# Scores of two head pairs, their transposes and the stream's transposes each issued at one place in a two-layer decoder trunk

## The chip, the cores and the metric

The kernel runs on one core of one Trainium2 chip, as one program. The metric is the device time of one execution in microseconds (us); before the change three runs took 2105.35 to 2106.36 us, with a median of 2105.8. The engines have these names in the profile: PE is TensorE's matmuls, PEld its weight loads, DVE is VectorE, ACT is ScalarE, POOL is GpSimd, SP the queue that issues the weights' transfers. Each engine takes its instructions in the order in which the program gives them to it.

## The reference

Two layers act on 256 tokens of 2048 numbers, each with a token mixer and an MLP, both behind a normalisation and added to the stream. Float32 throughout.

```python
for i in range(2):
    h = rmsnorm(x, norm_mix[i])
    if i == 0:
        x = x + sliding_window_sink_attention(h, a_w_qkv[0], a_w_o[0], a_sinks[0])   # 32 heads, 4 key heads
    else:
        x = x + stick_breaking_attention(h, b_w_qkv[0], b_w_o[0])                     # 32 heads
    h = rmsnorm(x, norm_mlp[i])
    x = x + (relu(h @ w_in[i]) ** 2) @ w_out[i]                                        # hidden 8192
return rmsnorm(x, final_norm)

# mixer A, head h, 128-query blocks that see their own and the previous key block
s = q @ k.T / 8 - slope[h] * dist;  m = max(max(s), sink)
p = exp(s - m) / (sum(exp(s - m)) + exp(sink - m));  out = p @ v

# mixer B, strictly causal
z = q @ k.T / 8;  a[t, s] = sigmoid(z[t, s]) * prod_{s<j<t} (1 - sigmoid(z[t, j]));  out = a @ v
```

## The kernel before

Tokens lie in two tiles of 128 (`xt`), and a transposed, gain-scaled copy of the stream (`xg`, sixteen tiles of 128 features by 256 tokens) feeds the projections. Every float32 operand is held as a rounded high half and a low half, the difference; a product is the sum of three matmuls over the halves. All weights pass through one `WeightStream`: a 1 MB transfer from the SP queue into `wraw`, then for each half of it a cast on ScalarE (line 67, the high half of `wsplit`) and a subtraction on VectorE (line 75, the low half). TensorE runs through the weights in order.

The order on TensorE, ScalarE and VectorE is written out by hand. A projection (`proj`, `proj_v`, `proj_wide`) is a loop of steps; after each step it calls `between()`, which runs the stages that `plan((place, stage), ...)` put at this place, counted from the step after the call, and then `W.tick()`, which at every fourth step issues the cast of the weights ahead and one step later its subtraction. A step of `proj` is four matmuls, 16 steps make one projection; a place in `proj_wide` is three matmuls 512 wide. So attention, normalisation and transposes are woven into the stream of the next projections, and what a stage issues on ScalarE or VectorE stands in these engines' queues behind all that came at earlier places.

Attention A: eight groups (n = 0 to 7), each of two head pairs, four heads. A group's queries come from one projection; `summed` (ScalarE copies `low`, line 331, VectorE adds), the row scale (`qf`), and the split `qhl` follow. The scores of a pair (`pair_scores`, lines 381 and 383) fill two banks; VectorE adds the distance penalty while it reads them (`sc`, line 488) and finds the maxima (492 to 499); ScalarE takes the exponentials (`powers`, 506 and 509); VectorE sums up (`total`); ScalarE normalises (520). `turned` transposes a head's probabilities on TensorE (`transposed`, line 390) and splits them from the bank into `pTa` (ScalarE cast, then VectorE at the next place). `values` multiplies with `vpad` (539) and splits the result into `attnT`. Transposes and values of group n run during the projection of group n + 2 (`older`).

Attention B: eight groups j of two pairs. Values, keys and queries are projected one after another, 48 steps. `scores` adds the causal mask in the bank (639), `gates` takes two sigmoids of each head on ScalarE, `stick` makes the products along the keys on VectorE (two scans and two multiplications a head, 655 and 657), `turned` transposes and splits into `pT`, `values` multiplies (672 to 675).

At the end of each wide chunk (`ended`) the residual is added and the stream's four new tiles are transposed (`turn`, lines 227 to 232). `token_scale` makes the row scale, and its `spread` (272) multiplies it across the partitions.

PSUM is eight banks: four (`m`) for projections, four (`s`) handed out in rotation for scores, transposes, values and the spread. An instruction that writes a bank waits until what was in it has been read.

## Time and profile before

| | value |
|---|---|
| median of three runs | 2105.8 us |
| the profiled execution | 2106.19 us |
| its span in the profile | 2104.4 us |
| PE busy | 2077.8 us, 99% |
| PEld busy | 1760.6 us, 84% |
| DVE busy | 1303.8 us, 62% |
| ACT busy | 1094.5 us, 52% |
| mean granted clock of TensorE | 0.998 |
| 100 to 200 us (attention A): PE, DVE, ACT | 95.82, 79.73, 75.69 of 100 us |
| 700 to 800 us (MLP): PE, DVE, ACT | 100.00, 64.34, 55.52 of 100 us |
| 1100 to 1200 us (attention B): PE, DVE, ACT | 100.00, 83.17, 58.20 of 100 us |

Attention A lies from about 50 to 200 us of the span, the first MLP from 284 to 983, attention B from there to 1310, the second MLP from 1398 on. A busy PE means that some matmul was in flight; matmuls overlap, so their cost is read from the distance of their starts. The same holds on ScalarE and VectorE, where an instruction may start some 0.1 us before the one ahead has ended.

### The profile page before, as it was taken

The numbers are of one execution on the slowest core, as the hardware profiler recorded it, in microseconds if no ns is written. First come the engines' busy times: TensorE is split into PE (matmuls) and PEld (weight loads), VectorE is DVE, ScalarE is ACT, GpSimd is POOL, SyncE is SP. The second block draws the span as 40 slices with busy tenths as digits, with TensorE's granted clock in tenths as the row PEclk, the third lists the DMA queues.
The fourth block names the chain that finished last, engine by engine and source line by source line (L and its number), as shares of the span: only waits on it lengthen the run. The fifth ranks groups of instructions, "written<-read, shape, count | busy, mean of one in ns | idle before, by whom it ended". The sixth has DMA issues, their size and how long they took to land.

```text
span 2104.4 us, 27478 instructions
## 1 busy us (share of the span) xinstructions
PE 2077.8 (99%) x10994; PEld 1760.6 (84%) x10994; DVE 1303.8 (62%) x1845; ACT 1094.5 (52%) x1771; POOL 7.4 (0%) x17
## 2 busy tenths in 40 slices
PE   8999999999999999999999999999999999999998
PEld 7777888888888888888888888888888888888886
DVE  5887566664446665555778788566664445665454
ACT  6776555553335554444555555455553335554443
POOL 0000000000000000000000000000000000000000
PEclk9999999999999999999999999999999999999999
DMA  8555866565565566555544554566656566566553
GB/s 228 133 121 121 185 196 197 182 199 187 196 196 181 184 200 194 186 181 195 165 162 158 168 166 147 189 193 199 188 183 205 186 198 187 180 193 200 192 189 119
DMA packets 340464, 380.37 MB, mean 181 GB/s; under 512 B 72624, under 2 KB 257008, under 8 KB 340208
## 3 DMA queue, kind: packets, MB, share of 16 engines
q1 hardware_dynamic: 339760, 376.50, 58.4%
q8 instruction: 86, 1.41, 0.3%
q10 hardware_dynamic: 576, 2.11, 0.2%
q14 instruction: 42, 0.34, 0.1%
HBM read 376.49 MB, written 2.10 MB: 180 GB/s over the span
## 4 chain that ended last, share of the span: by engine, by line
PE 91%; DVE 4%; ACT 3%; DMA 1%; issue 1%; SPq 0%; ACTq 0%; DVEq 0%
PE m L291 43%; PE m L300 41%; PE m L323 5%; DVE wsplit L75 1%; DMA wraw<-in_a_w_qkv_dram 1%; ACT sc L520 1%; ACT wsplit L67 1%; ACT sc L506 1%; PE s L390 1%; PE s L227 0%; DVE sc L488 0%; PE s L381 0%; DVE mx L492 0%; PE s L672 0%; DVE t L333 0%
## 5 line engine op out<-in xcount | busy, mean ns | idle before, releaser
L75 DVE TENSOR_TENSOR wsplit<-wraw,wsplit 128x1024 fp32r<-128x1024 f32 x712 | 857.8, 1223 | 531.2 <-ACT wsplit L67 530.8
L67 ACT CAST wsplit<-wraw 128x1024 fp32r<-128x1024 f32 x712 | 732.6, 1051 | 581.1 <-PE m L300 421.9
L291 PE MATMUL m<-xg,wsplit 128*128 128x256 f32 (+1 forms) x5696 | 1016.5, 338 | 3.3 <-DVE wsplit L75 2.8
L291 PEld LDWEIGHTS m<-xg,wsplit 128*128 128x128 f32 x5696 | 861.5, 188 | 125.5 <-DVE wsplit L75 3.2
L300 PE MATMUL m<-wsplit,h 128*128 128x512 f32 x3072 | 699.9, 389 | 0.0
L300 PEld LDWEIGHTS m<-wsplit,h 128*128 128x128 f32 x3072 | 575.7, 188 | 119.0
L300 PE MATMUL m<-wsplit,attnT 128*128 128x512 f32 x768 | 184.6, 395 | 0.0
L300 PEld LDWEIGHTS m<-wsplit,attnT 128*128 128x128 f32 x768 | 142.2, 189 | 28.2 <-issue 0.2
L341 DVE TENSOR_TENSOR h<-hsq,h 128x256 fp32r<-128x256 f32 x128 | 54.5, 425 | 118.1 <-ACT h L338 118.1
L331 ACT COPY low<-m 128x256 f32<-128x256 f32 x178 | 63.4, 370 | 122.7 <-PE m L291 122.5
L577 ACT ACTIVATE hsq<-t 128x256 f32<-128x256 f32 x128 | 53.5, 418 | 126.7 <-DVE t L575 126.7
L333 DVE TENSOR_TENSOR t<-m,low 128x256 f32<-128x256 f32 x178 | 73.0, 421 | 62.3 <-ACT low L331 62.2
L323 PE MATMUL m<-wsplit,xg 128*128 128x256 f32 (+1 forms) x576 | 110.8, 343 | 0.0
L323 PEld LDWEIGHTS m<-wsplit,xg 128*128 128x128 f32 x576 | 85.1, 188 | 11.4
L575 DVE SCALAR_TENSOR_TENSOR t<-t,rbc 128x256 f32<-128x256 f32 x128 | 54.4, 425 | 4.4
L338 ACT CAST h<-hsq 128x256 fp32r<-128x256 f32 x128 | 52.0, 406 | 4.1
L229 ACT ACTIVATE xg<-s,gains 128x256 fp32r<-128x256 f32 x64 | 28.6, 474 | 31.0 <-PE s L227 30.7
L232 DVE SCALAR_TENSOR_TENSOR xg<-s,gains,xg 128x256 fp32r<-128x256 f32 x64 | 29.3, 480 | 23.0 <-ACT xg L229 23.0
L506 ACT ACTIVATE sc<-sc,nm 128x256 f32<-128x256 f32 x64 | 28.4, 445 | 23.0 <-DVE nm L497 22.3
L366 DVE TENSOR_TENSOR xt<-m,xt 128x512 f32<-128x512 f32 x46 | 29.8, 684 | 15.6 <-PE m L300 15.6
L243 ACT ACTIVATE junk<-xt 128x512 f32<-128x512 f32 x40 | 25.1, 628 | 23.0 <-DVE xt L366 11.5
L655 DVE TENSOR_TENSOR_SCAN rest<-keep 128x256 f32<-128x256 f32 x64 | 35.3, 551 | 0.0
(106 smaller groups left out, 641.0 us busy)
## 6 DMA issues: line engine op xcount, KB each, us to landing
wraw<-in_mlp_w_in_dram SPq DMA_DIRECT2D x128, 1024.0 KB, 5.7
wraw<-in_mlp_w_out_dram SPq DMA_DIRECT2D x128, 1024.0 KB, 5.0
wraw<-in_b_w_qkv_dram SPq DMA_DIRECT2D x48, 1024.0 KB, 5.0
wraw<-in_a_w_qkv_dram SPq DMA_DIRECT2D x64, 256.0 KB, 3.9
wraw<-in_a_w_o_dram SPq DMA_DIRECT2D x32, 512.0 KB, 7.0
wraw<-in_b_w_o_dram SPq DMA_DIRECT2D x16, 1024.0 KB, 5.0
wraw<-in_a_w_qkv_dram SPq DMA_DIRECT2D x3, 1024.0 KB, 10.0
xt<-in_x_dram SPq DMA_DIRECT2D x4, 256.0 KB, 4.8
```

Of the source, the lines that this page charges most:

```text
L67: self.nc.scalar.copy(out=wt[:, 0], in_=raw)
L75: self.nc.vector.tensor_tensor(out=wt[:, 1], in0=raw, in1=wt[:, 0].bitcast(F32), op=ALU.subtract)
L291: nc.tensor.matmul(banks[j][:, :cols], lhsT=wt[:, u, kt % UK, j * P : (j + 1) * P], rhs=act[:, kt, : cols // S, :], start=(kt == 0 and u = ...
L300: nc.tensor.matmul(banks[tt], lhsT=act[:, kt, a, tt * P : (tt + 1) * P], rhs=wt[:, w, kt % 2, :], start=(first and n == 0), stop=(last and ...
L323: nc.tensor.matmul(banks[tt][:, :cols], lhsT=act[:, kt, u, tt * P : (tt + 1) * P], rhs=wt[:, : cols // S, kt % UK, :], start=(kt == 0 and ...
L331: nc.scalar.copy(out=low, in_=b[:, S:])
L333: nc.vector.tensor_add(out=t, in0=b[:, :S], in1=low)
L338: nc.scalar.copy(out=hi, in_=src)
L341: nc.vector.tensor_tensor(out=lo, in0=src, in1=hi.bitcast(F32), op=ALU.subtract)
L506: nc.scalar.activation(out=sc[:, hh, cols], in_=sc[:, hh, cols], func=AF.Exp, bias=nm[:, hh, blk : blk + 1], scale=1.0, accum_out=den[:, h ...
L575: nc.vector.scalar_tensor_tensor(out=t, in0=t, scalar=0.0, in1=scale["row"], op0=ALU.max, op1=ALU.mult)
L577: nc.scalar.activation(out=sq, in_=t, func=AF.Square)
```

## The change

Five things are rearranged, and no arithmetic is added or taken away.

1. `pair_scores` takes both pairs: the split products of both, then the full-precision products of both. It allocates four banks at once. In A the scores of both pairs stand at place 5 (before: 3 and 6, both 3 in the last group); `scores` is divided into `distances`, which runs at once for both pairs, and `maxima`, at places 6 and 7. In B the scores stand at place 4 (before 3 and 4, both 3 in the last group).
2. The four transposes of a group's probabilities stand at one place: in A at 9 (before 1, 1, 7, 8), in B at 18 (before 12, 13, 18, 20). Values: A 14 as before, B both at 24 (before 20, 24).
3. Four stream tiles are transposed at one place of the next chunk, 4 (before one each at 3, 4, 5, 6), two to a bank; at the start two each at places 0 to 5 (before one each at 0 to 11).
4. The last groups' places are further apart: A own transposes at 15 and values at 20 (before 10, 12, 13, 13 and 18); B 14 and 20 (before 11, 12, 15, 16 and 16, 18).
5. The spread stands five places after the row scale (before four).

The core of the diff:

```diff
-    def turn(dt, gain, wait):
-        b = bank("s", 4)
-        for tt in range(2):
-            nc.tensor.transpose(b[:, tt * P : (tt + 1) * P], xt[tt][:, dt * P : (dt + 1) * P], ident)
...
+    def turn(dts, gain, wait):
+        banks = [bank("s", 4) for _ in dts[::2]]
+        parts = [banks[n // 2][:, n % 2 * S : n % 2 * S + S] for n in range(len(dts))]
+        for dt, b in zip(dts, parts):
+            for tt in range(2):
+                nc.tensor.transpose(b[:, tt * P : (tt + 1) * P], xt[tt][:, dt * P : (dt + 1) * P], ident)
...
+            if wait:
+                plan((n // 2, lambda dt=dt, b=b: low(dt, b)))
...
-        plan((4, spread))
+        plan((5, spread))
...
-        for n in range(4):
-            plan((3 + n, lambda n=n: turn(4 * c + n, gain, True)))
-        plan((2, lambda: square(0, c)), (4, lambda: square(1, c)))
+        plan((2, lambda: square(0, c)), (3, lambda: square(1, c)),
+             (4, lambda: turn(range(4 * c, 4 * c + 4), gain, True)))
...
+    def pair_scores(*pairs):
+        banks = [[bank("s", 4) for _ in range(2)] for _ in pairs]
+        rows = [slice(hh * HD, (hh + 1) * HD) for hh in range(2)]
+        for (qf, q, kf, k), bs in zip(pairs, banks):
+            for n, (u, v) in enumerate(((0, 0), (1, 0), (0, 1))):
+                for r, b in zip(rows, bs):
+                    nc.tensor.matmul(b[:, :S], lhsT=q[r, u, P:], rhs=k[r, v, :], start=(n == 0), stop=(n == 2))
+        for (qf, q, kf, k), bs in zip(pairs, banks):
+            for r, b in zip(rows, bs):
+                nc.tensor.matmul(b[:, S : S + P], lhsT=qf[r, :P], rhs=kf[r, :P], start=True, stop=True)
+        return banks
...
             if older:
-                plan(*zip((1, 1, 7, 8, 14) if n < 7 else (0, 3, 3, 6, 12), older))
+                plan(*zip((9, 14), older))
+            plan((5, scores))
             if n < 7:
-                plan(*zip((3, 6, 7, 13), pair[0][0]), *zip((6, 10, 13, 14), pair[1][0]))
+                plan(*zip((6, 8, 9, 12), pair[0][1]), *zip((7, 11, 13, 15), pair[1][1]))
             else:
-                plan(*zip((3, 4, 5, 6), pair[0][0]), *zip((3, 6, 8, 11), pair[1][0]), *zip((10, 12, 13, 13, 18), late))
+                plan(*zip((6, 7, 8, 10), pair[0][1]), *zip((7, 9, 11, 12), pair[1][1]), *zip((15, 20), late))
...
+            plan((4, scores))
             if j < 7:
-                plan(*zip((3, 5, 9, 10, 12, 13, 20), a), *zip((4, 9, 12, 12, 18, 20, 24), b))
+                plan(*zip((5, 9, 10), pairs[0][1]), *zip((9, 12, 13), pairs[1][1]), (18, turns), (24, both_values))
             else:
-                plan(*zip((3, 5, 5, 6, 11, 12, 16), a), *zip((3, 5, 7, 9, 15, 16, 18), b))
+                plan(*zip((5, 7, 8), pairs[0][1]), *zip((6, 9, 10), pairs[1][1]), (14, turns), (20, both_values))
```

What it does to the queues, first on ScalarE in a middle group of attention A. Before, from one group's `low` on, the rows are (`L338` are splits, `L67` weight casts, `L506` exponentials of the first pair):

```order
L331 COPY low<-m 128x256 x2
L338 CAST qhl<-qf 128x256 x2
L67 CAST wsplit<-wraw 128x1024
L338 CAST pTa<-s 128x3x128 x2
L67 CAST wsplit<-wraw 128x1024
L506 ACTIVATE sc,den<-sc,nm 128x256
L506 ACTIVATE sc,den<-sc,nm 128x128
L506 ACTIVATE sc,den<-sc,nm 128x256
L506 ACTIVATE sc,den<-sc,nm 128x128
L509 ACTIVATE es<-es 128x4
L338 CAST pTa<-s 128x3x128 x2
L67 CAST wsplit<-wraw 128x1024
```

and now, with the lines renumbered (`L341` splits, `L513` exponentials):

```order
L334 COPY low<-m 128x256 x2
L341 CAST qhl<-qf 128x256 x2
L67 CAST wsplit<-wraw 128x1024 x2
L513 ACTIVATE sc,den<-sc,nm 128x256
L513 ACTIVATE sc,den<-sc,nm 128x128
L513 ACTIVATE sc,den<-sc,nm 128x256
L513 ACTIVATE sc,den<-sc,nm 128x128
L516 ACTIVATE es<-es 128x4
L67 CAST wsplit<-wraw 128x1024
L341 CAST pTa<-s 128x3x128 x4
```

Two probability casts stood ahead of the second weight cast and two behind the exponentials; now all four stand behind the exponentials and one more weight cast.

On VectorE in the same group before (`L75` low halves of weights, `L488` distance passes, `L492` to `L499` maxima, `L341` low halves of probabilities):

```order
L75 TENSOR_TENSOR wsplit<-wraw,wsplit 128x1024
L341 TENSOR_TENSOR pTa<-s,pTa 128x3x128 x2
L488 SCALAR_TENSOR_TENSOR sc<-dist,s 128x384 x2
L492 TENSOR_REDUCE mx<-sc 128x6
L493 TENSOR_TENSOR mx<-mx 128x2
L497 SCALAR_TENSOR_TENSOR nm<-mx,nsinks 128x4
L499 TENSOR_TENSOR es<-nm,nsinks 128x4
L75 TENSOR_TENSOR wsplit<-wraw,wsplit 128x1024
L488 SCALAR_TENSOR_TENSOR sc<-dist,s 128x384 x2
L492 TENSOR_REDUCE mx<-sc 128x6
```

and now (`L492` distance passes, `L499` to `L506` maxima):

```order
L75 TENSOR_TENSOR wsplit<-wraw,wsplit 128x1024
L492 SCALAR_TENSOR_TENSOR sc<-dist,s 128x384 x4
L75 TENSOR_TENSOR wsplit<-wraw,wsplit 128x1024
L499 TENSOR_REDUCE mx<-sc 128x6
L500 TENSOR_TENSOR mx<-mx 128x2
L504 SCALAR_TENSOR_TENSOR nm<-mx,nsinks 128x4
L506 TENSOR_TENSOR es<-nm,nsinks 128x4
L499 TENSOR_REDUCE mx<-sc 128x6
L500 TENSOR_TENSOR mx<-mx 128x2
L504 SCALAR_TENSOR_TENSOR nm<-mx,nsinks 128x4
L506 TENSOR_TENSOR es<-nm,nsinks 128x4
L520 TENSOR_TENSOR den<-den,es 128x4
```

Four distance passes and a weight half stand ahead of the first maximum, and the probabilities' low halves, ahead of the distances before, come three rows after the last one shown.

On TensorE at the end of attention B before (`L381` and `L383` scores, `L390` transposes, `L672` values, `L300` the output projection):

```order
L300 MATMUL m<-wsplit,attnT 128x512 x12
L381 MATMUL s<-khl,qhl 128x256 x6
L383 MATMUL s<-kf,qf 128x128 x2
L381 MATMUL s<-khl,qhl 128x256 x6
L383 MATMUL s<-kf,qf 128x128 x2
L300 MATMUL m<-wsplit,attnT 128x512 x24
L390 MATMUL s<-ident,beta 128x128 x3
L300 MATMUL m<-wsplit,attnT 128x512 x3
L390 MATMUL s<-ident,beta 128x128 x3
L300 MATMUL m<-wsplit,attnT 128x512 x9
L390 MATMUL s<-ident,beta 128x128 x3
L300 MATMUL m<-wsplit,attnT 128x512 x3
```

and now (`L385` and `L388` scores, `L395` transposes, `L690` values, `L303` the output projection):

```order
L303 MATMUL m<-wsplit,attnT 128x512 x15
L385 MATMUL s<-khl,qhl 128x256 x12
L388 MATMUL s<-kf,qf 128x128 x4
L303 MATMUL m<-wsplit,attnT 128x512 x30
L395 MATMUL s<-ident,beta 128x128 x12
L303 MATMUL m<-wsplit,attnT 128x512 x18
L690 MATMUL s<-pT,vpad_8158 128x512
```

The four transposes of probabilities stand together behind thirty matmuls, and the values eighteen later.

## Rows read from the trace of the kernel before

**Rows 1.** Waits of TensorE: waiter, releaser, us in total, times, longest.
```profile
PE s L381 <- ACT qhl L338: 4.1, 7, 1.2
...
PE s L672 <- DVE pT L341: 1.2, 1, 1.2
...
PE s L272 <- DVE diag L267: 0.7, 2, 0.4
```

**Rows 2.** Timeline of one group of attention A: start, duration, engine, line, instruction.
```profile
101.93 0.62 ACT L331 COPY low<-m 128x256 f32<-128x256 f32 x2
...
104.08 1.04 ACT L67 CAST wsplit<-wraw 128x1024 fp32r<-128x1024 f32 x1
...
105.15 1.23 DVE L75 TENSOR_TENSOR wsplit<-wraw,wsplit 128x1024 fp32r<-128x1024 f32 x1 [0.52 <-ACT wsplit L67]
...
106.30 1.01 DVE L341 TENSOR_TENSOR pTa<-s,pTa 128x384 fp32r<-128x384 f32 x2
107.23 1.01 DVE L488 SCALAR_TENSOR_TENSOR sc<-dist,s 128x384 f32<-128x384 f32 x2
...
109.65 0.51 ACT L506 ACTIVATE sc<-sc,nm 128x256 f32<-128x256 f32 x1 [2.83 <-DVE nm L497]
...
111.52 0.83 ACT L338 CAST pTa<-s 128x384 fp32r<-128x384 f32 x2
...
112.25 1.05 ACT L67 CAST wsplit<-wraw 128x1024 fp32r<-128x1024 f32 x1
...
115.30 1.03 ACT L67 CAST wsplit<-wraw 128x1024 fp32r<-128x1024 f32 x1
...
117.63 0.56 ACT L338 CAST attnT<-s 128x512 fp32r<-128x512 f32 x1
118.10 1.49 ACT L520 ACTIVATE sc<-sc,den 128x256 f32<-128x256 f32 x4
...
119.50 0.62 ACT L331 COPY low<-m 128x256 f32<-128x256 f32 x2
```

**Rows 3.** Chain of waits, MLP stretches: start, duration, what, count.
```profile
1567.57 174.09 PE m L300 x768
1741.66 178.35 PE m L291 x1024
```

**Rows 4.** Stretches: length, busy (x count) of PE, PEld, DVE, ACT, POOL, PEclk, DMA.
```profile
174.00:178.00 4.00, 2.35 (x17) 1.79 (x19) 3.09 (x6) 1.50 (x5) 0.00 (x0) 0.91 0.24 46
178.00:182.00 4.00, 4.00 (x19) 3.13 (x16) 3.76 (x12) 2.90 (x10) 0.00 (x0) 0.67 0.00 0
1304.00:1308.00 4.00, 2.81 (x18) 2.15 (x17) 3.97 (x7) 0.48 (x1) 0.00 (x0) 1.00 0.05 19
```

**Rows 5.** TensorE's timeline in a group of attention B, scores.
```profile
1020.35 0.63 PE L381 MATMUL s<-khl,qhl 64*128 64x256 f32 x6
...
1022.03 0.62 PE L381 MATMUL s<-khl,qhl 64*128 64x256 f32 x6
```

**Rows 6.** Timeline at the end of attention B, TensorE.
```profile
1293.86 0.62 PE L381 MATMUL s<-khl,qhl 64*128 64x256 f32 x6
...
1300.78 0.49 PE L390 MATMUL s<-ident,beta 128*128 128x128 f32 x3
```

**Rows 7.** TensorE's timeline in the output projection of attention A.
```profile
189.63 0.82 PE L390 MATMUL s<-ident,sc 128*128 128x128 f32 x6
...
193.70 2.25 PE L539 MATMUL s<-pTa,vpad 128*128 128x512 f32 x12
...
207.37 0.38 PE L227 MATMUL s<-ident,xt 128*128 128x128 f32 x2
...
208.30 0.38 PE L227 MATMUL s<-ident,xt 128*128 128x128 f32 x2
```

**Rows 8.** Timeline at the end of attention B, VectorE.
```profile
1296.81 0.69 DVE L655 TENSOR_TENSOR_SCAN rest<-keep 128x256 f32<-128x256 f32 x1
...
1298.54 1.22 DVE L75 TENSOR_TENSOR wsplit<-wraw,wsplit 128x1024 fp32r<-128x1024 f32 x1
```

More of the change, by code (lines that the diff above doesn't have):

```diff
@@ L468, in trunk_kernel @@
             gains_in(0)
[L469 to L471 removed]
+            turn(range(4), 0, False)
+            plan(*[(n, lambda n=n: turn(range(4 + 2 * n, 6 + 2 * n), 0, True)) for n in range(6)],
                  *[(12 + c, lambda c=c: square(0, c)) for c in range(4)])
@@ L483, in head_pair, with distances @@
             blocks = (slice(0, S), slice(S, S + P))
-            def scores():
+            def distances(banks):
                 sc = st["sc"] = tmp.tile([P, 2, 3 * P], F32, name="sc", bufs=4)
-                for hh, b in enumerate(pair_scores(qf, q, kf[:, gp, :], k[:, gp])):
+                for hh, b in enumerate(banks):
                     nc.vector.scalar_tensor_tensor(out=sc[:, hh, :], in0=dist,
@@ L524, in turned @@
                 transposed(st["sc"][:, hh, :], pTs[hh][:, 0, :, u, :], pTs[hh][:, 1, :, u, :])
-            return (scores, powers, total, normalise), turned
+            return distances, (maxima, powers, total, normalise), turned
         def values(pTs, gp, i):
@@ L680, in values @@
                      (1, lambda: split(attnT[:, 2 * j + u, 0, :], attnT[:, 2 * j + u, 1, :], t, 0)))
-            return scores, gates, lambda: stick(0), lambda: stick(1), lambda: turned(0), lambda: turned(1), values
+            return masked, (gates, lambda: stick(0), lambda: stick(1)), turned, values
         for j in range(8):
@@ L690, in trunk_kernel, with scores, turns, both_values @@
             qs = scaled(tmp, proj(NDT, xg), r8, "q")
-            a, b = [head_pair(j, u, ks[u], qs[u]) for u in range(2)]
+            pairs = [head_pair(j, u) for u in range(2)]
+            def scores(ks=ks, qs=qs, pairs=pairs):
+                made = pair_scores(*[(*qt, *kt) for qt, kt in zip(qs, ks)])
+                for (masked, _, _, _), banks in zip(pairs, made):
+                    masked(banks)
+            def turns(pairs=pairs):
+                for _, _, turned, _ in pairs:
+                    for hh in range(2):
+                        turned(hh)
+            def both_values(pairs=pairs):
+                for _, _, _, values in pairs:
+                    values()
+            plan((4, scores))
             if j < 7:
-                plan(*zip((3, 5, 9, 10, 12, 13, 20), a), *zip((4, 9, 12, 12, 18, 20, 24), b))
+                plan(*zip((5, 9, 10), pairs[0][1]), *zip((9, 12, 13), pairs[1][1]), (18, turns), (24, both_values))
             else:
-                plan(*zip((3, 5, 5, 6, 11, 12, 16), a), *zip((3, 5, 7, 9, 15, 16, 18), b))
+                plan(*zip((5, 7, 8), pairs[0][1]), *zip((6, 9, 10), pairs[1][1]), (14, turns), (20, both_values))
         out_proj(attnT, 3)
```

48 lines of the change are left out of this document (22 added, 26 removed).

## The prediction

> **What bounds the kernel now.** I read the slices of the page first: TensorE is busy and at full granted clock in every slice, so most of the span is a matmul stream with other work beside it. The waits of TensorE come next [rows 1]: few and short, and the only repeated one stands in attention A, where the scores wait for the split queries seven times. Then one group of A in time order [rows 2]: the same ScalarE copy (`low`) stands at 101.93 and at 119.50, so a group lasts 17.57 us. TensorE's own work does not fill that: sixteen steps of four matmuls at 178.35/256 = 0.697 [rows 3] are 11.15, four score and transpose insertions and one set of value products about 5.5, together 16.7. The rows name what does fill it: each starts where one before it ended, ScalarE and VectorE in turn. In A the group is a closed loop through the two in-order queues of ScalarE and VectorE, and TensorE has 0.9 us to spare. In the MLPs and in attention B the opposite holds: 768 matmuls in 174.09 us without a break [rows 3], and in the steady B loop no wait at all (the 1.2 us for `pT` [rows 1] is the end of B).
>
> **Group A, which decides.** The change lets both pairs' scores, all four distance passes and then both maxima go one after the other on VectorE, and puts all four probability casts in one block on ScalarE, behind the first pair's exponentials. No instruction is added or removed there; what changes is who stands behind whom. I rebuild the loop from [rows 2] in the new order, from `low` to the next `low`: to the first weight cast 104.08 - 101.93 = 2.15; until its VectorE half 1.07; that half 1.15; four distance passes at the rate of two 384-wide passes in 107.23 - 106.30 = 0.93, so 1.86; the next weight half, which stands between them and the maxima, 1.15; maxima until the exponentials, 109.65 - 107.23 less two passes, 1.49; exponentials of the first pair 111.52 - 109.65 = 1.87; a weight cast, 117.63 - 115.30 = 2.33 less the four normalisations 119.50 - 118.10 = 1.40, so 0.93; four probability casts at 0.73 for two, 1.46; exponentials of the second pair 1.87; normalisation and weight cast 2.33; `attnT` cast 0.47; second normalisation 1.40. Sum 19.20, against 17.57: +1.63 a group. Before, two of the casts stood early, while ScalarE had nothing to do until the maxima, and the second pair's distances and maxima ran beside the first pair's exponentials; now ScalarE idles over all four distance passes and then has 3.3 us of queue before the second pair's exponentials. Six such loops give +9.8. The first has no older probabilities (1.46 + 0.47 less), its excess lies between 0 and 1.6, I take 0.8: **+10.6**.
>
> Does TensorE hide it? The values at place 14 need the third low half of the probabilities. Counted from `low`: exponentials end at 10.74, the weight cast's half may start at 11.81, ends at 12.96, three lows end at about 14.4. TensorE leaves the previous values (1.75 after their wait) at 14.4 + 1.75 - 19.2 = -3.0, seven steps (4.88) bring it to the scores at 1.8, which end at about 3.4; nine steps and twelve transposes (6.27 + 1.32) bring it to the values at 11.0. It waits there about 3 us, with two matmuls in between. The old wait of the scores for the split queries goes (most of the 4.1 us in [rows 1]), but a new one of the values for VectorE's `pTa` is late next, and longer. Behind the waiting value product stand the rest of its own matmuls, a step, and the next group's scores, which still arrive 1.0 before VectorE can take them (4.37): so the loop, not TensorE, keeps the time.
>
> **End of A.** Before, the stretch 174 to 178 had TensorE idle for 4.00 - 2.35 = 1.65 and the clock's fall cost (1 - 0.91) x 4 + (1 - 0.67) x 4 = 1.7 [rows 4]; both go with the later scores. New: the older values wait about 2.4 by the same queue; and the transposes of the fourth own head take, by the rotation of four banks, the bank of those values, whose low half on VectorE waits behind a weight half; that ends near 19.7 where TensorE is there at 17.2, so 2.6. +5.0 - 3.35 - 0.5 for merged insertions = +1.1; bounds -2 and +3, the bank order being read from the code alone; I take **+0.8**.
>
> **The merged insertions.** One pair's scores: 1022.03 - 1020.35 less one step 0.70 = 0.98 [rows 5]; two pairs at once: 1300.78 - 1293.86 less 24 x 174.09/768 = 5.44, so 1.48 [rows 6]. Merging saves 0.48 wherever TensorE keeps the time: not in A. Six transposes cost 193.70 - 189.63 less 15 x 0.227 = 0.67, two cost 208.30 - 207.37 less 0.68 = 0.25 [rows 7]: 0.11 each and 0.01 to 0.03 for entering. So grouping transposes saves next to nothing: eight together 0.89 against 1.00, for twelve ends of wide chunks 1.3 by the rounded rows, of which I take **-1.0**. The run of six in these rows costs no more for each transpose than the run of two, so no clock was lost over it. The Trainium skill ("TensorE: Matmul & The Clock Gate", Part 4: PE-mode transpose) says otherwise: that the full clock does not engage for transposes, and that one took about 275 ns in a kernel's context. By that figure twelve are, as an estimate, 3.3 us where the rows give 1.3; what the rule would do here is rival four.
>
> **Start and row scales.** Six insertions of four transposes for twelve of two save about 0.3; the tiles turned earlier also spare TensorE a wait for a late half. Bounds -2 and +0.5, I take -0.7. The sums' spread, one place later, gets 0.7 us more cover: the two waits of 0.7 in all [rows 1] go. Together **-1.4**.
>
> **Group B.** Merged scores save 0.48 a group. The transposes move from places 12 to 20 to place 18, the values to 24. VectorE after the scores: four masks (1.4, an estimate at the 384-wide rate scaled down), four weight halves 4.6, four sticks at 1298.54 - 1296.81 = 1.73 [rows 8] 6.9, the two value inputs and their halves with one wait for ScalarE 2.5, then the first low half 0.5: 15.9. TensorE reaches the values after 20 x 0.697 + 1.32 = 15.3. A new wait of about 0.5 eats the 0.48: **0**, bounds -3.5 (no wait) and +3.5 (a wait of 1). In the last group the transposes come ten places of 0.68 after the scores, at 6.8, and the fourth is at the array at 8.0, but the fourth stick ends at 1.3 + 2 x 1.15 + 6.9 = 10.5: a wait of 2.6, in place of the 1.2 of [rows 1]: +1.4, merging -0.2, **+1.2**.
>
> **The clock.** It fell once, from 2.4 to 1.2 GHz, after TensorE had stood idle for 1.65 of 4 us, and it did not at the end of B, after 1.19 of idling [rows 4]. The new waits are longer than both. A fall costs 1.7 of TensorE's time; in the A loop 1.0 of it is covered, so 0.7 each. Six there and three at the ends are between 0 and +9.3; when a fall comes I can't tell, I take **+2**.
>
> Sum: 10.6 + 0.8 - 1.0 - 1.4 + 0 + 1.2 + 2 = **+12.2**. The profiled execution took 2106.2 us (span 2104.4), 0.4 above the median; so 2118.4 on its own, 2118.0 for a median.
>
> **Rivals.**
> One, faster: the A loop is closed by TensorE after all, at 11.15 + 1.48 + 1.32 + 2.1 = 16.05, because the new order lets the two queues run ahead. Then A gains 1.5 x 7, B 0.48 x 7, start and turns 2.4: 2090. The 4.1 us that go [rows 1] speak for it; against it, TensorE already had spare time while the loop took 17.57. It decides if the values do not wait. Chance 0.07.
> Two, about the same: the A loop grows by only half (part of the casts slips into ScalarE's idle time), B's values don't wait: +5.3 - 3.4 + 0.6 = 2108.5. The long idle of ScalarE before its exponentials speaks for it; the order of the queue against. 0.15.
> Three, much slower: the clock falls at every new wait, +9.3 in place of +2: 2125. For it, the new waits are longer than the one at which it fell; against it, each is split by two matmuls. 0.20.
> Four, slower still: a run of twelve transposes brings the clock down by itself. There are eight such runs in B, where nothing covers a fall: 8 x 1.7 = 13.6 more, 2132. Against it stands the run of six [rows 7]. 0.03. This is what the Trainium skill's section on transposes, cited above, would do here.
>
> **How the numbers follow.** The forecast keeps 0.55, with its own range 2112 to 2123. The range runs from 2107 to 2127: it holds the forecast, rival three and most of two, and leaves out one, four and the ends of the others, about 0.18. What a measurement of this kernel can tell from no change is 0.2%, 4.2 us: slower than 2110.0 is the forecast, rival three and a small part of two, 0.80; faster than 2101.6 is rival one and a little, 0.08; between, 0.12.
>
> **What would show it.** After: `low` to `low` in A at 19 rather than 17.6; TensorE waiting for `pTa` in the line of the value products, six or seven times, 2 to 3.5 each, and no longer for `qhl`; in B nothing over 1 until the last group, where transposes wait for `beta`. A period of 17.6 or less, or value products that start at once, would make it wrong; so would B groups shorter than before by 0.4 or more.

## The result, and the profile after

The changed kernel takes 2121.7 us (median of four runs, 2121.12 to 2121.94) against 2105.9 in the same measurement: ratio 1.0075, 95% interval 1.0064 to 1.0087. It is slower, 3.7 us more than the forecast and inside its own range. The profiled execution has a span of 2120.0 us, 15.7 more than before, at a mean granted clock of 0.993 (0.998).

Where it went can be read exactly, since the matmuls on the weights' stream are the same 10112 in the same order in both traces. The starts of the same matmul, after less before, at the borders of the stages:

| stage | us longer (after less before) | forecast |
|---|---|---|
| up to the first product | +1.49 | start -0.7 |
| keys and values of A | -0.56 | |
| the eight query projections, with A's loop woven in | +13.84 | +10.6, and most of the clock's +2 |
| first chunk of A's output projection | +2.03 | +0.8 |
| from there to the first product of B | -1.17 | chunk ends -1.0, spread -0.7 (both layers) |
| B, eight groups | -0.93 | 0 |
| first chunk of B's output projection | +1.18 | +1.2 |
| the rest | -0.22 | (chunk ends, as above) |
| sum (before rounding) | +15.67 | +12.2 |

TensorE's waits after (waiter, releaser, us in total, times, longest), to be held against [rows 1]:

```profile
PE s L546 <- DVE pTa L344: 10.9, 11, 2.0
...
PE m L294 <- DVE wsplit L75: 4.3, 1, 4.3
PE s L385 <- ACT qhl L341: 3.2, 1, 3.2
PE s L395 <- DVE attnT L344: 2.6, 1, 2.6
PE s L395 <- DVE beta L675: 2.3, 1, 2.3
```

The seven waits of the scores for `qhl` are down to one; eleven records of value products that wait for `pTa` stand in their place. The wait at the start has grown from 2.8 to 4.3, the one at the end of B from 1.2 to 2.3, and at the end of A there is a new one of 2.6. A middle group of A, the counterpart of [rows 2]:

```profile
89.34 0.63 ACT L334 COPY low<-m 128x256 f32<-128x256 f32 x2
...
93.72 1.94 DVE L492 SCALAR_TENSOR_TENSOR sc<-dist,s 128x384 f32<-128x384 f32 x4
...
98.08 0.51 ACT L513 ACTIVATE sc<-sc,nm 128x256 f32<-128x256 f32 x1 [4.59 <-DVE nm L504]
...
100.89 1.59 ACT L341 CAST pTa<-s 128x384 fp32r<-128x384 f32 x4
...
102.37 0.52 ACT L513 ACTIVATE sc<-sc,nm 128x256 f32<-128x256 f32 x1
...
102.86 0.59 PE L546 MATMUL s<-pTa,vpad 128*128 128x512 f32 x2 [1.98 <-DVE pTa L344]
...
108.43 0.64 ACT L334 COPY low<-m 128x256 f32<-128x256 f32 x2
```

From `low` to `low` 19.09, where it was 17.57. The first exponentials (`L513`) start 8.74 after `low`; before it was 7.72. Ahead of them VectorE makes four distance passes (93.72), behind them stand a weight cast, all four probability casts (100.89) and only then the second pair's exponentials (102.37). TensorE waits 1.98 for the casts' low halves at its value products (102.86). All eight `low` stand at 51.94, 70.27, 89.34, 108.43, 128.01, 147.60, 166.70 and 186.16. From the second `low` on these are six steady loops; the first group is a case of its own. Three of the six are 19.07 to 19.10, three 19.46 to 19.59; in each of these three the clock fell once (near 122.2, 142.7 and 180.2). Stretches (length, PE, PEld, DVE, ACT, POOL busy with counts, granted clock, DMA):

```profile
118.00:122.00 4.00, 2.02 (x12) 1.44 (x11) 2.93 (x9) 4.00 (x15) 0.00 (x0) 1.00 0.31 69
122.00:126.00 4.00, 3.92 (x13) 3.00 (x14) 1.76 (x6) 3.75 (x13) 0.00 (x0) 0.57 0.96 218
207.50:211.00 3.50, 3.50 (x10) 2.71 (x9) 1.96 (x3) 0.94 (x1) 0.00 (x0) 0.51 0.94 229
1000.00:1300.00 300.00, 299.73 (x1843) 259.78 (x1842) 238.54 (x425) 172.59 (x308) 2.19 (x2) 1.00 0.51 165
```

After TensorE had been busy for 2.02 of 4 us the clock was at 1.2 GHz for most of the next four (0.57), and so again at the end of A (0.51). In B it stays at 1.00.

### The profile page after: what moved, and what is told of

Same layout as the page of the kernel before. It is cut to its first block, busy times and chain, and to the rows that moved or that the text cites. A ratio compares the mean times of both kernels' runs of the same rounds, so it can differ in the third digit from the quotient of the medians.

```text
span 2120.0 us, 27530 instructions
## 1 busy us (share of the span) xinstructions
PE 2080.4 (98%) x10994; PEld 1768.5 (83%) x10994; DVE 1301.1 (61%) x1845; ACT 1093.9 (52%) x1771; POOL 7.4 (0%) x17
## 4 chain that ended last, share of the span: by engine, by line
PE 92%; ACT 3%; DVE 3%; issue 1%; DMA 0%; SPq 0%; ACTq 0%; DVEq 0%
PE m L294 43%; PE m L303 40%; PE m L326 5%; DVE wsplit L75 1%; ACT sc L513 1%; ACT wsplit L67 1%; ACT sc L527 1%; PE s L230 1%; DVE sc L492 1%; PE s L546 1%; PE s L690 0%; PE s L395 0%; PE s L385 0%; DVE mx L499 0%; DVE t L336 0%
## 5 line engine op out<-in xcount | busy, mean ns | idle before, releaser
L75 DVE TENSOR_TENSOR wsplit<-wraw,wsplit 128x1024 fp32r<-128x1024 f32 x712 | 857.2, 1223 | 535.5 <-ACT wsplit L67 527.5
L67 ACT CAST wsplit<-wraw 128x1024 fp32r<-128x1024 f32 x712 | 731.4, 1052 | 575.2 <-PE m L303 422.8
L303 PE MATMUL m<-wsplit,h 128*128 128x512 f32 x3072 | 697.8, 389 | 0.0
L303 PEld LDWEIGHTS m<-wsplit,h 128*128 128x128 f32 x3072 | 576.4, 188 | 119.6
L303 PE MATMUL m<-wsplit,attnT 128*128 128x512 f32 x768 | 179.6, 393 | 0.0
L303 PEld LDWEIGHTS m<-wsplit,attnT 128*128 128x128 f32 x768 | 144.4, 189 | 29.9
L326 PE MATMUL m<-wsplit,xg 128*128 128x256 f32 (+1 forms) x576 | 104.7, 339 | 0.0
L341 ACT CAST h<-hsq 128x256 fp32r<-128x256 f32 x128 | 52.0, 406 | 4.1
L513 ACT ACTIVATE sc<-sc,nm 128x256 f32<-128x256 f32 x64 | 28.4, 450 | 37.2 <-DVE nm L504 37.2
L546 PE MATMUL s<-pTa,vpad 128*128 128x512 f32 (+1 forms) x96 | 24.6, 406 | 11.0 <-DVE pTa L344 10.9
```

The source lines that it names most:

```text
L67: self.nc.scalar.copy(out=wt[:, 0], in_=raw)
L75: self.nc.vector.tensor_tensor(out=wt[:, 1], in0=raw, in1=wt[:, 0].bitcast(F32), op=ALU.subtract)
L303: nc.tensor.matmul(banks[tt], lhsT=act[:, kt, a, tt * P : (tt + 1) * P], rhs=wt[:, w, kt % 2, :], start=(first and n == 0), stop=(last and ...
L326: nc.tensor.matmul(banks[tt][:, :cols], lhsT=act[:, kt, u, tt * P : (tt + 1) * P], rhs=wt[:, : cols // S, kt % UK, :], start=(kt == 0 and ...
L341: nc.scalar.copy(out=hi, in_=src)
L513: nc.scalar.activation(out=sc[:, hh, cols], in_=sc[:, hh, cols], func=AF.Exp, bias=nm[:, hh, blk : blk + 1], scale=1.0, accum_out=den[:, h ...
```

## The experiments

The theory: in attention A the order of work in the queues of ScalarE and VectorE closes the loop, and everything TensorE does or waits for there follows from it. The rivals: the falls of the clock and TensorE's waits make the loss; or the merged blocks themselves (twelve transposes, four banks at once) do. Up to the run on the start and the ends, the edits shown are against the changed kernel, from there on against the run before; "..." marks lines left out. "Period" is the time from `low` to `low` in the steady groups.

**A's order of before.**

```diff
...
-                plan(*zip((9, 14), older))
-            plan((5, scores))
+                plan(*zip((1, 1, 7, 8, 14) if n < 7 else (0, 3, 3, 6, 12), older))
             if n < 7:
-                plan(*zip((6, 8, 9, 12), pair[0][1]), *zip((7, 11, 13, 15), pair[1][1]))
+                plan((3, lambda s=scores: s(0)), *zip((3, 6, 7, 13), pair[0][1]),
+                     (6, lambda s=scores: s(1)), *zip((6, 10, 13, 14), pair[1][1]))
...
```

The last group has its old places too.

> The changed kernel with attention A alone put back: scores of one pair at a time at places 3 and 6, each head's transposes at its own place (1, 1, 7, 8), the last group's places of before; start, stream transposes, spread and attention B stay changed. Theory (the order of work in the queues of ScalarE and VectorE closes A's loop): the period from one `low` to the next falls from 19.1 to 19.6 back to 17.55, the last group's excess of 2.0 goes, and the time is 2121.7 - 13.9 - 2.0 = 2105.8 (2105 to 2107). Rival (a good part of the loss comes from the start, from the stream transposes or from a clock fall that these parts set off): A's period stays above 18 or the time stays above 2110.

Measured 2106.7 us, ratio to the kernel before 1.0003 (0.9994 to 1.0013). Period 17.48 to 17.58 (before 17.47 to 17.57), A's stage +0.43 instead of +13.84, the first chunk of its output projection -1.19 instead of +2.03. The -1.19 goes with the clock: this run's trace has no fall there, the trace before has one, reckoned at 1.7. All of the loss is in A's order; what the start costs, the other parts give back.

**The transposes at 7.**

```diff
-                plan(*zip((9, 14), older))
+                plan(*zip((7, 14), older))
```

> The changed kernel with one number of attention A changed: the older group's four transposes stand at place 7 instead of 9, so that their casts stand ahead of the first pair's exponentials in ScalarE's queue instead of behind them. The work on every engine, the banks and the run of twelve transposes are the same. Theory: ScalarE idles there for 4.6 us, so the 1.46 of casts cost nothing any more; exponentials still start 8.7 after `low`; period 19.1 - 1.46 = 17.6, TensorE's waits for `pTa` go, clock falls in A become fewer; six loops give -8.7 and the falls some -1: 2112 (2110.5 to 2113.5). Rival one (the block of twelve transposes or its four banks cost the time): period 19 or more, 2121. Rival two (the waits of TensorE and the falls of its clock make the loss): the period hardly moves unless the falls go, and then by 0.4 a group: 2119.

Measured 2110.4 us (ratio 1.0017, 1.0008 to 1.0027), at the lower edge of what was expected. ScalarE in a middle group:

```profile
107.02 0.62 ACT L334 COPY low<-m 128x256 f32<-128x256 f32 x2
...
112.72 1.74 ACT L341 CAST pTa<-s 128x384 fp32r<-128x384 f32 x4 [1.55 <-PE s L395]
115.77 0.51 ACT L513 ACTIVATE sc<-sc,nm 128x256 f32<-128x256 f32 x1 [1.31 <-DVE nm L504]
...
124.63 0.62 ACT L334 COPY low<-m 128x256 f32<-128x256 f32 x2
```

Same blocks, same banks, one number: the casts now lie at 112.72, in ScalarE's idle time, the exponentials start 8.75 after `low` as before the edit, and five of the six periods are 17.60 to 17.61, the forecast value; the other, 18.45, holds the only fall of the clock in A. TensorE still waits, 7.3 us in six waits for `qhl`, while 11 us are gone from the time: its waits are no measure of the loss. Nor is it the clock: the loops without a fall take 19.09 and 19.10 in the changed kernel and 17.61 here. The rival of the merged transposes falls.

**The scores apart, the transposes together at 9.**

```diff
...
-            plan((5, scores))
             if n < 7:
-                plan(*zip((6, 8, 9, 12), pair[0][1]), *zip((7, 11, 13, 15), pair[1][1]))
+                plan((3, lambda s=scores: s(0)), *zip((3, 6, 9, 12), pair[0][1]),
+                     (6, lambda s=scores: s(1)), *zip((6, 11, 13, 15), pair[1][1]))
...
```

> The changed kernel with attention A's scores taken apart again (one pair at place 3, one at 6, each followed at once by its distances and maxima), in groups 0 to 6; the four transposes stay together at place 9, values at 14. Theory: the first exponentials start when one pair's distances and maxima are done, 6.8 after `low` (before 7.7 with two low halves of the probabilities in between), then 1.87 + 0.93 + 1.46 of casts + 1.87 + 4.3 to the next `low`: period 17.2 (17.0 to 17.7). Six loops of -1.9 and the clock falls of A, some -1.3, less: 2121.7 - 11.4 - 1.3 = 2109 (2107 to 2112). Rival (the casts in one block behind the exponentials cost the time, whatever the scores do): period 18.1 to 18.6, 2115 to 2117.

Measured 2110.1 us (1.0018, 1.0008 to 1.0027). ScalarE:

```profile
105.27 0.62 ACT L334 COPY low<-m 128x256 f32<-128x256 f32 x2
...
112.06 0.51 ACT L513 ACTIVATE sc<-sc,nm 128x256 f32<-128x256 f32 x1 [2.65 <-DVE nm L504]
```

The first exponentials start 6.79 after `low`, as reckoned, and four of the six steady periods are 17.44 to 17.52; 17.87 and 18.89 stand beside them, the latter with a fall of the clock. That is 0.3 above the 17.2 reckoned: TensorE enters the loop here, where the `attnT` cast waits up to 0.6 for the values. So the block of four casts behind the exponentials is harmless as soon as the exponentials start early.

This trace is of the slowest of the ten executions (2112.6), and 1.6 of it are lost at the end of B, which the edit doesn't touch. There TensorE waits for `beta` as in the changed kernel, and of the six traces with that wait this is the only one in which the clock falls behind it. The same eighteen matmuls, first in the changed kernel, then here, with the wait ahead of them and the clock (columns as in the stretches above):

```profile
1321.47 4.36 PE L303 MATMUL m<-wsplit,attnT 128*128 128x512 f32 x18
```

```profile
1310.16 0.52 PE L395 MATMUL s<-ident,beta 128*128 128x128 f32 x3 [2.34 <-DVE beta L674]
1310.44 5.96 PE L303 MATMUL m<-wsplit,attnT 128*128 128x512 f32 x18
...
1311.00:1314.50 3.50, 3.50 (x10) 2.69 (x9) 3.15 (x6) 1.24 (x2) 0.00 (x0) 0.55 0.56 170
```

**The transposes apart, the scores together.**

```diff
...
-                plan(*zip((9, 14), older))
+                plan(*zip((1, 1, 7, 8, 14) if n < 7 else (9, 9, 9, 9, 14), older))
...
```

> The changed kernel with the older group's transposes of attention A put back to places 1, 1, 7, 8 (groups 0 to 6), the scores still together at place 5. With the kernels that have been run this fills the table of scores (apart or together) against transposes (apart or together at 9). Theory: all four casts then stand ahead of the first exponentials, but two of their low halves (0.93) stand ahead of the four distance passes on VectorE: exponentials at 4.36 + 0.93 + 1.95 + 1.15 + 1.3 = 9.7 after `low`, then 1.87 + 0.94 + 1.87 + 4.2 to the next one: period 18.6 (18.3 to 19.0), only 0.5 shorter than in the changed kernel; 2117 (2114 to 2119). Rival (the transposes in one block behind the exponentials are the fault and the scores together are harmless): period 17.6 or less, 2110.

Measured 2128.0 us (1.0103, 1.0089 to 1.0117): 9 slower than the theory allows, and its step failed. The six steady periods are 19.45 and 19.46 where the clock stays up, 20.30 and 20.31 with one fall in the loop, 21.39 and 21.61 with a longer one. One row of the waits, and a group at full clock:

```profile
PE s L385 <- DVE pTa L344: 11.5, 6, 2.0
```

```profile
133.31 0.62 ACT L334 COPY low<-m 128x256 f32<-128x256 f32 x2
...
138.29 1.08 PE L385 MATMUL s<-ka,qhl 64*128 64x256 f32 x6 [1.87 <-DVE pTa L344]
...
139.52 1.95 DVE L492 SCALAR_TENSOR_TENSOR sc<-dist,s 128x384 f32<-128x384 f32 x4 [0.81 <-PE s L388]
...
142.82 0.48 ACT L341 CAST pTa<-s 128x384 fp32r<-128x384 f32 x1 [0.56 <-PE s L395]
143.89 0.51 ACT L513 ACTIVATE sc<-sc,nm 128x256 f32<-128x256 f32 x1 [0.59 <-DVE nm L504]
...
152.76 0.63 ACT L334 COPY low<-m 128x256 f32<-128x256 f32 x2
```

I had counted VectorE's queue alone. Four score banks at once are all four of the rotation, so the second pair's scores wait for the banks of the two transposes ahead until VectorE has read these (138.29 instead of 136.42). The distances start 6.21 after `low` instead of 5.3, the exponentials at 10.6 instead of 9.7, and the period is 19.45 where I had 18.6. Taking the scores together costs the banks as well as VectorE's order. The rest is the clock. In the group from 113.00 to 133.31 it fell:

```profile
120.00:123.40 3.40, 3.40 (x13) 2.78 (x12) 3.33 (x7) 0.48 (x1) 0.00 (x0) 0.53 0.98 220
```

There the later transposes run at half speed, and the last cast, directly ahead of the exponentials, comes 11.1 after `low` (at 124.08) instead of 9.5:

```profile
124.08 0.48 ACT L341 CAST pTa<-s 128x384 fp32r<-128x384 f32 x1 [1.13 <-PE s L395]
```

**The values at 16.**

```diff
-                plan(*zip((9, 14), older))
+                plan(*zip((9, 16 if n < 7 else 14), older))
```

> The changed kernel with the older group's values of attention A at place 16 (the first of the next projection) instead of 14, groups 0 to 6. It takes away TensorE's repeated wait for `pTa` (10.9 us in all) by putting two more steps between transposes and values. Theory: that wait is a symptom; the loop through ScalarE and VectorE gets only the `attnT` cast out (0.47, into ScalarE's idle 0.9 before the split queries) and some 0.1 of `attnT`'s low half in: period 19.08 - 0.4 = 18.7 (18.5 to 19.1), and TensorE waits the same 2 to 3 a group at the scores, for `qhl`: 2119 (2116 to 2121). Rival (the wait at the values is what the change lost): without it the period falls to 17.0 to 17.6, 2109 to 2111.

Measured 2117.2 us (1.0054, 1.0039 to 1.0070). Period 18.61 in all steady loops. The waits:

```profile
PE s L385 <- ACT qhl L341: 7.4, 7, 3.3
...
PE s L546 <- DVE pTa L344: 3.9, 12, 1.3
PE s L385 <- DVE qhl L344: 2.7, 6, 0.5
```

10.9 of waiting for `pTa` have become 3.9, and the scores wait 7.4 and 2.7 for `qhl` instead: the wait moves, the loop stays. A's stage is 9.0 shorter than in the changed kernel and the first chunk behind it 4.7 longer, but this is mostly the border between them: 3.1 are the older values with their waits, which place 16 moves into the chunk, 1.6 the scores of the last group, which wait there for `qhl`. Both stretches together are 4.3 shorter.

**Start and ends.**

```diff
             if wait:
                 plan((n // 2, lambda dt=dt, b=b: low(dt, b)))
-            else:
+        if not wait:
+            for dt, b in zip(dts, parts):
                 low(dt, b)
...
-                plan(*zip((6, 7, 8, 10), pair[0][1]), *zip((7, 9, 11, 12), pair[1][1]), *zip((15, 20), late))
+                plan(*zip((6, 7, 8, 10), pair[0][1]), *zip((7, 9, 11, 12), pair[1][1]), *zip((19, 24), late))
...
-                plan(*zip((5, 9, 10), pairs[0][1]), *zip((9, 12, 13), pairs[1][1]), (18, turns), (24, both_values))
+                plan(*zip((5, 9, 10), pairs[0][1]), *zip((9, 12, 13), pairs[1][1]), (18, turns), (26, both_values))
             else:
-                plan(*zip((5, 7, 8), pairs[0][1]), *zip((6, 9, 10), pairs[1][1]), (14, turns), (20, both_values))
+                plan(*zip((5, 7, 8), pairs[0][1]), *zip((6, 9, 10), pairs[1][1]), (17, turns), (22, both_values))
```

> The changed kernel with four edits in four separate stretches, each read by itself from where the same matmul of the weights' stream starts. (1) Start: the four casts of the first stream tiles first, then their four low halves, with the same two banks. Theory: ScalarE's second and fourth cast wait for VectorE's low half of the tile that shares the bank (idle 0.55 and 0.58 before them); first product at 10.1 to 10.3 instead of 11.6, -1.4. Rival: the casts wait for the transposes of the shared bank, then -0.4 or less. (2) End of A: own transposes at 19 instead of 15, values at 24 instead of 20. Theory: the wait of 2.6 for the bank of the older values goes, -2.0 to -2.6. Rival: `attnT` comes too late for the output projection's last product, then the wait only moves. (3) B, groups 0 to 6: values at 26 instead of 24; they entered 0.18 later than free ones and cost 0.27 more a group: -1.9 in all, 0 if it is not a wait. (4) End of B: transposes at 17 instead of 14, values 22 instead of 20: the wait of 2.3 for `beta` becomes 0.3, -2.0. Sum -7.5: 2114 (2112.5 to 2116.5).

Measured 2111.8 us (1.0030, 1.0019 to 1.0040), 0.7 below the range expected. The start in three kernels, before, changed and edited, on ScalarE (in the first two also TensorE's first product):

```profile
6.03 1.75 ACT L229 ACTIVATE xg<-s,gains 128x256 fp32r<-128x256 f32 x4 [3.36 <-PE s L227]
...
10.11 1.65 PE L291 MATMUL m<-xg,wsplit 128*128 128x256 f32 x4 [2.84 <-DVE wsplit L75]
```

```profile
6.45 0.47 ACT L237 ACTIVATE xg<-s,gains 128x256 fp32r<-128x256 f32 x1 [3.77 <-PE s L230]
...
7.47 0.84 ACT L237 ACTIVATE xg<-s,gains 128x256 fp32r<-128x256 f32 x2 [0.55 <-DVE xg L233]
...
8.89 0.47 ACT L237 ACTIVATE xg<-s,gains 128x256 fp32r<-128x256 f32 x1 [0.58 <-DVE xg L233]
...
11.61 1.22 PE L294 MATMUL m<-xg,wsplit 128*128 128x256 f32 x3 [4.34 <-DVE wsplit L75]
```

```profile
6.36 1.69 ACT L237 ACTIVATE xg<-s,gains 128x256 fp32r<-128x256 f32 x4 [3.69 <-PE s L230]
```

In the changed kernel the second and fourth cast each wait for VectorE's low half of the tile in the same bank; four casts ahead of four low halves run without a gap, and the first product comes at 10.30 instead of 11.61. From the start of the first cast to that of the first product it is 5.16 or 5.17 in all six kernels with the changed kernel's start, 3.94 to 4.33 in the others (4.08 before), so the order costs 1.1. The rest of the changed kernel's +1.49 is that its first cast started 0.4 later; this start lies anywhere from 5.8 to 7.2 in these traces, whatever the edit. The keys' stretch is 0.9 shorter too, but it is 0.8 shorter in the run with the values at 16 as well, whose start is not edited, so that is not shown to be the edit. At the end of A, TensorE in the changed kernel and in the edited one:

```profile
202.73 1.14 PE L395 MATMUL s<-ident,sc 128*128 128x128 f32 x9
206.43 0.55 PE L395 MATMUL s<-ident,sc 128*128 128x128 f32 x3 [2.56 <-DVE attnT L344]
```

```profile
203.01 1.50 PE L396 MATMUL s<-ident,sc 128*128 128x128 f32 x12
```

The wait of 2.56 for the bank of the older values is gone; the chunk gets 3.97 shorter, 1.4 more than the wait, and the half-speed stretch at 207.5 is gone with it. B's groups get 0.28 shorter each (they are 0.41 below before instead of 0.13), B's end 2.03. The start and both parts in B came out as reckoned; the end of A gave 1.4 more than the 2.0 to 2.6 expected, since I had left out the clock.

**Putting it together.** A's order as in the first run, B's places (18 and 26, 17 and 22) as in the one above, and the start's first tiles one by one:

```diff
-            turn(range(4), 0, False)
+            for dt in range(4):
+                turn((dt,), 0, False)
...
```

> The kernel with A's order of before and the rest changed, and in it what the run of the start and ends showed: at the start the first four tiles turned one by one in banks of their own as before, in B the values at 26, in B's last group transposes at 17 and values at 22. From 2106.7: start -1.7 (first product back at 10.1), B seven times -0.28, B's end -2.0: 2101 (2099.5 to 2102.5). Rival (B's later values delay the next group's projections through VectorE, or the start's loss is in the pairs of tiles that follow): 2103 or more.

Measured 2100.6 us (0.9975, 0.9965 to 0.9984). From here on only A's places differ, in the tuple of `older` (transposes, values) and in the place of the second pair's scores and maxima (the first of the steady loops is 18.2 to 18.3 in the first two rows, with a fall of the clock, and 16.1 in the last two):

| run | older transposes, values | second scores | period | us | ratio to before |
|---|---|---|---|---|---|
| put together | 1, 1, 7, 8, 14 | 6 | 17.57 | 2100.6 | 0.9975 (0.9965 to 0.9984) |
| transposes 5 | 1, 1, 5, 5, 14 | 6 | 17.57 | 2100.4 | 0.9974 (0.9964 to 0.9984) |
| scores 5, transposes 6 | 1, 1, 6, 6, 14 | 5 | 17.45 | 2098.3 | 0.9965 (0.9953 to 0.9978) |
| both 5 | 1, 1, 5, 5, 14 | 5 | 17.70 | 2100.3 | 0.9973 (0.9963 to 0.9983) |
| values 17 | 1, 1, 5, 5, 17 | 5 | 17.05 | 2097.2 | 0.9958 (0.9945 to 0.9970) |
| values 16 | 1, 1, 5, 5, 16 | 5 | 16.53 | 2093.4 | 0.9940 (0.9926 to 0.9953) |

```diff
-                plan(*zip((1, 1, 7, 8, 14) if n < 7 else (0, 3, 3, 6, 12), older))
+                plan(*zip((1, 1, 5, 5, 14) if n < 7 else (0, 3, 3, 6, 12), older))
```

> As the kernel before it in this set, and in attention A the older group's third and fourth transposes at place 5 instead of 7 and 8 (ahead of the second pair's scores). Theory: their two casts (0.73) move from behind the first exponentials into the 2.8 us in which ScalarE waits for the maxima: period 17.55 - 0.7 = 16.85 (16.7 to 17.1), TensorE being nearly as long by then; six loops -4.3: 2097 (2095.5 to 2099). Rival one (TensorE's wait for the banks of the first scores, read at 6.3 after `low`, holds up everything behind it): period 17.5 or more, 2101. Rival two (longer idling brings the clock down in each group): 2099 to 2101 with falls in the clock's rows.

A miss: the period did not move. ScalarE:

```profile
126.27 0.94 ACT L341 CAST pTa<-s 128x384 fp32r<-128x384 f32 x2 [0.67 <-PE s L395]
...
132.21 0.51 ACT L514 ACTIVATE sc<-sc,nm 128x256 f32<-128x256 f32 x1 [0.88 <-DVE nm L505]
```

The two casts moved as meant (126.27), but the second exponentials (132.21) then idled 0.88 for VectorE: its second maxima, behind a weight half, ended where they had ended before. Two chains of the same length stood side by side, and I had followed only ScalarE's.

```diff
-                plan(*zip((1, 1, 5, 5, 14) if n < 7 else (0, 3, 3, 6, 12), older))
+                plan(*zip((1, 1, 6, 6, 14) if n < 7 else (0, 3, 3, 6, 12), older))
...
-                     (6, lambda s=scores: s(1)), *zip((6, 10, 13, 14), pair[1][1]))
+                     (5, lambda s=scores: s(1)), *zip((5, 10, 13, 14), pair[1][1]))
```

> As the kernel before it in this set, but the second pair's scores at place 5 and the older third and fourth transposes behind them at place 6: TensorE then finds the banks free, but the weights' low half on VectorE stands behind the second maxima and the casts end some 0.3 after the first exponentials could start. Theory: period 17.1 (16.8 to 17.4), 2098.5 (2097 to 2100.5). Rival (TensorE closes the loop by now and the order of the queues no longer matters): the same time as the kernel before it, within 0.5.

The second distances go ahead of that weight half: 17.45, not the 17.1 hoped for. Its time came out for other reasons: against the run put together, the first group got 1.0 shorter (15.21 from 16.19), and the second loop 0.8, mostly because the clock did not fall there in this trace. The five others gained only 0.1 each.

With 5, 5 for 6, 6 in that tuple:

> As the run with the second scores at 5 and the older transposes at 6 (2098.3), but both at place 5, the transposes ahead. Theory: the casts of the probabilities end 0.9 earlier on ScalarE, so the first exponentials start when the maxima are done (7.7 after `low` instead of 8.3); TensorE, which held up the `attnT` cast by 0.17 there, closes the loop by then: period 17.1 (16.9 to 17.45), six loops -2: 2096 (2094.5 to 2098.3). Rival (TensorE was closing the loop already): the same, 2098.3.

A miss, 2 slower than the run before it; the intervals overlap, but the period says the same. One row of ScalarE:

```profile
134.04 0.59 ACT L341 CAST attnT<-s 128x512 fp32r<-128x512 f32 x1 [0.98 <-PE s L547]
```

The `attnT` cast waits 0.98 for the value products, and the second normalisation and `low` stand behind it. TensorE has got into the loop by this one cast.

With 17 for 14 in it:

> As the run with older transposes and second scores at place 5 (2100.3, period 17.7), and the older values at place 17, the second of the next projection, in groups 0 to 6. Theory: there the loop was closed through TensorE: the `attnT` cast, which waits 1.0 for the values, stands on ScalarE ahead of the second normalisation and so ahead of the next `low`. At 17 the cast stands behind `low`, the split queries and a weight cast, where ScalarE idles; its low half (0.68) on VectorE comes ahead of the first distances. Exponentials at 7.7 + 0.7 = 8.4, then 1.87 + 0.94 + 1.87 + 0.94 + 2.8: period 16.8; TensorE's own work is 16.7, so 17.0 (16.8 to 17.4); seven groups of -0.7: 2095.5 (2093.5 to 2098). Rival (TensorE itself is full at 17.7 in this order, its steps being longer than counted): 2100.

As expected: 17.05. With 16:

> The same with the older values at place 16. Theory: the `attnT` cast then stands ahead of the split queries, and these are 1.5 to 2 later after `low`, since the cast must wait for the values on TensorE: period 17.8 (17.3 to 18.3), 2101 (2098 to 2104), slower than with place 17 by 3 to 8. Rival (which of the two places does not matter, since TensorE keeps the time in both): within 0.5 of the run with place 17.

Wrong way round, 8 below what I expected, and the best of all: 2093.4. TensorE's values and ScalarE in one group:

```profile
113.43 2.27 PE L547 MATMUL s<-pTa,vpad 128*128 128x512 f32 x12
114.26 0.62 ACT L334 COPY low<-m 128x256 f32<-128x256 f32 x2
...
115.73 0.59 ACT L341 CAST attnT<-s 128x512 fp32r<-128x512 f32 x1 [0.85 <-PE s L547]
...
116.22 0.71 ACT L341 CAST qhl<-qf 128x256 fp32r<-128x256 f32 x2
...
130.81 0.62 ACT L334 COPY low<-m 128x256 f32<-128x256 f32 x2
```

I had let the projection end with `low`. But ScalarE reaches `low` late (114.26) and TensorE is ahead of it by then: the values end in time for the cast to stand in ScalarE's idle 0.85 before the split queries. These come 1.96 after `low` instead of 1.51, and TensorE does not wait for them: it waits for nothing in these groups any more, its own work fills the loop of 16.53. That is the 16.7 that the prediction had reckoned for it, less 0.2.

## Why the prediction was right, and where its terms were off

By the table, the stages miss their terms by +1.6 (start and keys), +1.2 (A with the clock), +1.2 (end of A), +0.3 (chunk ends and spread) and -0.9 (B), in all 3.5 of a change of 15.7. Little of it cancels, so the hit does not rest on errors that offset each other.

- **The A loop, right.** 19.20 was reckoned from the rows of before in the new order; 19.09 and 19.10 were measured at full clock (19.07 with a fall that was covered), so +1.52 a loop against +1.63. The value products do wait for `pTa`, 2.2 a group where I said about 3, and two runs show that this wait is a symptom: moved to `qhl` it leaves the loop (18.61), and with one number changed the loop is back at 17.61 with waits left.
- **The first group, outside its bounds.** "I take 0.8", between 0 and 1.6; it was 2.1 (18.33 for 16.19, from `low` to `low`). Without older work TensorE is what comes last there: scores at place 5 reach VectorE late, which stood idle for 1.09 before its first distance pass. I applied the steady loop to a group that doesn't have it. TensorE then ran ahead and waited 3.2 for `qhl` in the second group, which I had said would not occur.
- **End of A, the new wait right, the rest off.** The wait for the bank, read from the code alone, was 2.6 as forecast. The older values waited 1.5, not 2.4. With these the term comes to +0.2. Most of the rest up to the measured +2.0 is the fall of the clock behind the wait, which was not in this term: 1.4, by what its removal gave.
- **The clock, mis-sized a little.** Five falls instead of one. Three cost a loop some 0.45 each (19.5 against 19.09), not 0.7; the one at 71.0, inside the wait of 3.2, lasted 6.8 us and left its loop at 19.07, being covered in whole; the one at the end of A cost 1.4, where nothing covers it. Rival three had one at each wait and in each loop.
- **The start, wrong in sign.** "Six insertions of four transposes for twelve of two save about 0.3" counts TensorE's side only. Two tiles in one bank, with each low half directly behind its cast, make ScalarE wait for VectorE: 1.1 of the +1.5 to the first product, the rest being a later first cast. The 1.1 comes back when the order is mended.
- **B, right in its parts.** By the starts of the stream's matmuls around them, the scores of two pairs cost 1.56 at once and 1.95 apart. So merging saves 0.39, not 0.48: the 1.48 was read at the end of B, among wide matmuls. Transposes and values together take 0.27 more, since the values wait; two places later this 0.27 comes back. I took the wait at 0.5 and the sum at 0; it was -0.13 a group. The end of B was +1.18 for a forecast of +1.2, and the wait for `beta` 2.3 for 2.6.
- **Rival four is out.** Four heads' transposes in B:

```profile
1125.84 1.47 PE L395 MATMUL s<-ident,beta 128*128 128x128 f32 x12
1127.07 4.44 PE L294 MATMUL m<-xg,wsplit 128*128 128x256 f32 x24
```

Twelve transposes hold TensorE for 1.31 by the starts around them, 0.11 each, at a granted clock of 1.00 over all of B. In the run with the transposes apart, three take 0.25 at full clock (141.25 to 141.50) and 0.49 in a half-speed stretch (121.59 to 122.08), so they follow the granted clock. The Trainium skill ("TensorE: Matmul & The Clock Gate", Part 4: PE-mode transpose) says that the full clock does not engage for them and gives about 275 ns for one. With the first this trace does not agree. The second agrees as the duration of one record (mean 273 ns here), but records overlap, so the estimate of 3.3 us for twelve in the prediction is not what they cost: it multiplies durations where the distance of the starts counts.

What is left open: when a wait brings the clock down. Waits of the same kind did and did not, the one for `beta` at the end of B (2.3) even with the same instructions around it. And each trace is of one execution, so a fall in it need not be in the others of that kernel.

## What to carry to other kernels

Where two in-order queues close a loop, rebuild the loop from the trace in the new order before touching places, and follow both queues and the third engine's work, which takes over when they get shorter (16.53): a cast belongs in the time in which its engine idles anyway, and a wait of TensorE does not by itself name what keeps the time. Merging operations paid where TensorE keeps the time (in B 0.41 a group, with the values two places later). Where the queues keep it, it brought nothing at best (17.61 against 17.57) and cost up to 1.9 a group (19.45), where the merged block takes every bank of the rotation at once. First and last groups have other neighbours than the steady ones and need a sum of their own.

## What the runs showed of the hardware that I had not expected

With the casts and low halves of two tiles in one bank issued in alternation, ScalarE's cast of the second tile started only when VectorE had read the first (idle 0.55 and 0.58); with one tile to a bank, or all casts first, four casts took 1.69 to 1.75 without a gap. The Trainium skill ("PSUM — Partial Sum Buffer", PSUM bank collisions raise a hardware error) says that the compiler's scheduler makes any two instructions of different engines that touch one bank in the same 32 partitions depend on each other, two readers too. The trace agrees with that (0.55 and 0.58 of waiting), and so it is where the low half stands in the program that costs the time. The first products stand 0.427 apart (two 512-wide matmuls, at 14.3 in the changed kernel, at 12.4 before) and later 0.23 (at 16.45, and 0.24 at 13.8), although the granted clock reads 1.00 in all these stretches: the slow start does not show in that column.
